# One visit to the values' products for four query blocks, with shared buffers in the first half

## The chip, the cores and the metric

The kernel runs on one core of a Trainium2 chip. The metric is the device time of one execution in microseconds (us); lower is better. Before the change the median of three runs is 1810.27 us (1809.09 to 1811.99).

## The reference, cut to what matters

The program is one layer of a hybrid decoder trunk on 1024 tokens of width 1024: an RWKV-7 branch, a stick-breaking attention, a cross-attention into 256 memory tokens, gates, an output projection and a convolutional feed-forward. The change touches the stick-breaking attention alone (8 heads of 64, blocks of 128 queries):

```python
for blk in range(t_len // SB_BLOCK):          # 8 blocks of 128 queries
    start = blk * SB_BLOCK; end = start + SB_BLOCK
    qb, kb, vb = q[:, :, start:end], k[:, :, :end], v[:, :, :end]
    z = jnp.einsum('bhqd,bhkd->bhqk', qb, kb) * scale
    mask = s_idx[None, :] < t_idx[:, None]
    log_1mb = jnp.where(mask, jax.nn.log_sigmoid(-z), 0.0)
    log_between = lax.cumsum(log_1mb, axis=3, reverse=True) - log_1mb
    attn = jnp.where(mask, jnp.exp(jax.nn.log_sigmoid(z) + log_between), 0.0)
    outs.append(jnp.einsum('bhqk,bhkd->bhqd', attn, vb))
```

The kernel uses that these weights telescope: it keeps the running products of 1 - sigmoid(z) and multiplies them with the differences of neighbouring values, so that a product with a plain causal triangle remains.

## The kernel before, in words

The method `sb_attn` (L895) runs 64 units: head pair p (4), head of the pair h2 (2), half of the blocks (0: blocks 0 to 3, 1: blocks 4 to 7), block in the half (4). Unit u works on query block b against (b+1)*128 keys. A unit passes four steps:

- `front` (L900): the products of queries and keys (two matrix products per 512 keys, hi and lo part) into a PSUM bank of the tag g, then ScalarE's sigmoid (L913) into a buffer sn of the tag at.
- `weigh` (L916): VectorE's scan (L919) in place over sn, the running product.
- `mid` (L921): TensorE transposes sn in blocks of 128x128 (L105) into g banks, and ScalarE copies them out (L931) into a second buffer of the tag at.
- `back` (L933): for two units at a time, TensorE multiplies the values' differences (64 columns as the stationary operand, so each product uses half of the array's columns) with the transposed weights. Unit i of the two writes the lower or upper 64 partitions of a PSUM bank py of the tag mm, so that the two can run side by side. Unit 1 of a visit has one key block more. When four blocks are done, ScalarE copies py out (L954, four instructions) and stores it.

The loop at L959 calls front(u), at even u back(u-4), then mid(u-2) and weigh(u). With `yield` it hands over to the filler: the program's large projections, one step per yield (six products of 512 columns into two mm banks, an eighth of a projection), woven in by `weave` (L1820) at a ratio of 1.03 to one. `pumped` (L1878) further mixes in the steps of `inverse` (L538), a long chain of VectorE multiplications and additions (L545, L547), which ends with eight-row stores from GpSimd's queue (L554).

Order. TensorE's instructions in this part are pinned to program order, as are VectorE's scans and the inverse's steps. ScalarE, GpSimd and the rest of VectorE are ordered by the tile scheduler from priorities and from when it believes operands to be ready, so an edit of the program order can move their instructions too. The pools hold: tag at, 7 buffers of 128x1024; mm, 4 PSUM banks; g, 4 PSUM banks; w4 (shown as w), 3 buffers; wr, wh and wl (raw, hi and lo part of a weight tile), 2 each.

The filler's gates matter below: when a gate's projection is done, ScalarE copies it out (L820), VectorE scales it (L821), and later `close` makes ScalarE apply a sigmoid in place (L824) and store it (L826). A weight tile is loaded by SP (L76), rounded by ScalarE (L80, wh) and its rest formed by GpSimd (L81, wl).

Of the kernel before, what the change touches and what calls it, by code (L numbers as in the profile page):

```python
# [49 lines left out]
class Trunk:  # L50
# [844 lines left out]
    def sb_attn(self, qk, need):  # L895
        nc = self.nc
        units = [(p, half, h2, half * 4 + bb) for p in range(4) for h2 in range(2) for half in range(2) for bb in range(4)]
        st = {}

        def front(u):  # L900
            p, half, h2, b = units[u]
            need(f"sb{p}")
            S, K, KL, nf = qk[p]
            W = (b + 1) * 128
            ts = slice(b * 128, (b + 1) * 128)
            sn = self.t4("at", n=1024)
            for w0 in range(0, W, 512):
                w1 = min(w0 + 512, W)
                pz = self.ps("g")
                self.mmul(pz[:, : w1 - w0], S[h2][:, ts], K[h2][:, w0:w1], start=True, stop=False)  # L910
                self.mmul(pz[:, : w1 - w0], S[h2][:, ts], KL[h2][:, w0:w1], start=False, stop=True)
                i = 2 * b + h2
                nc.scalar.activation(sn[:, w0:w1], pz[:, : w1 - w0], AF.Sigmoid, scale=nf[:, i : i + 1])  # L913
            st[u] = sn

        def weigh(u):  # L916
            W = (units[u][3] + 1) * 128
            sn = st[u]
            self.pinned(nc.vector.tensor_tensor_scan(sn[:, :W][:, ::-1], sn[:, :W][:, ::-1], self.nrt[:, 1152 - W :][:, ::-1], 1.0, ALU.mult, ALU.max))  # L919

        def mid(u):  # L921
            b = units[u][3]
            W = (b + 1) * 128
            at, sn = self.t4("at"), st[u]
            st[u] = at
            for w0 in range(0, W, 512):
                w1 = min(w0 + 512, W)
                pt = self.ps("g")
                for o in range(w0, w1, 128):
                    self.transpose(pt[:, o - w0 : o - w0 + 128], sn[:, o : o + 128])  # L930
                nc.scalar.activation(at[:, w0:w1], pt[:, : w1 - w0], AF.Copy)  # L931

        def back(u):  # L933
            p, half, h2, b = units[u]
            ats = [st.pop(u + i) for i in range(2)]
            if b % 4 == 0:
                st["py"] = self.ps("mm")
            py = st["py"]
            ts = slice(b % 4 * 64, b % 4 * 64 + 128)
            for j in range(b + 2):  # L940
                vo = (j % 2) * 512 + p * 128 + h2 * 64
                for i, at in enumerate(ats):
                    if j <= b + i:
                        self.mmul(
                            py[i * 64 : i * 64 + 64, ts], self.v[j // 2][:, vo : vo + 64], at[:, j * 128 : (j + 1) * 128],
                            start=(j == 0), stop=(j == b + i))
            if b % 4 == 2:
                q = slice(h2 * 64, h2 * 64 + 64)
                y = self.t4("ys", n=512)
                for i in range(2):  # L950
                    rows = slice(i * 64, i * 64 + 64)
                    for bb in range(2):
                        o, bi = (2 * bb + i) * 128, (2 * p + h2) * 4 + half * 2 + bb
                        nc.scalar.activation(  # L954
                            y[q, o : o + 128], py[rows, bb * 128 : bb * 128 + 128], AF.Identity,
                            bias=self.vlast[rows, bi : bi + 1])
                nc.scalar.dma_start(self.yd[1, p, q, half * 512 : (half + 1) * 512], y[q])

        for u in range(len(units) + 4):  # L959
            if u < len(units):  # L960
                front(u)
            if u % 2 == 0:
                yield
                if u >= 4:
                    back(u - 4)
            if 2 <= u < len(units) + 2:
                mid(u - 2)
            if u < len(units):
                weigh(u)
            yield  # L970
            if u % 2:
                yield
# [1017 lines left out]
```

## Time and profile before

| what | value |
|---|---|
| median of three runs | 1810.27 us |
| the profiled execution's own time | 1808.94 us |
| its span on the core | 1807.2 us |
| granted TensorE clock in it | 1.00 |
| TensorE busy | 1783.0 us, 99% of the span |
| VectorE, ScalarE, GpSimd busy | 65%, 48%, 44% |

The attention of the change lies between 324 and 634 us of the span. In the rows of the profile, PE is TensorE's products, PEld its weight loads, DVE VectorE, ACT ScalarE, POOL GpSimd, SP the engine that issues most transfers. A row of the timeline has the start, the length, the engine, the line, the operation, the tiles written and read, the shape, and in brackets the engine's idle time before it and what ended that. Lengths of overlapping products add up to more than the time that they take, so spacing between starts is what counts on PE.

### The profile page before, as it was taken

The page shows a single profiled execution, that of the slowest core. Times are in us where ns is not written, and L with a number is a line of the kernel's source. Part 1 is how long each engine was busy: PE and PEld are TensorE (multiplying, and loading weights), DVE is VectorE, ACT ScalarE, POOL GpSimd, SP SyncE. Part 2 cuts the span into 40 slices and gives each one's busy share as a digit, 9 for nine tenths or more (in the row PEclk, how much of TensorE's full clock was granted, in tenths as well). Part 3 has the DMA queues.
Part 4 walks back from the last instruction along what each step waited for, and adds up shares of the span by engine and source line. Part 5 has one row for each costly group of instructions (what it writes and reads, how often), then busy time and mean ns, then how long its engine had stood idle before and what let it go on. Part 6 is the DMA issues. An engine that isn't in the chain of part 4 may idle for free. (4 is left out here: it accounts for less than half of the span.)

```text
span 1807.2 us, 27322 instructions
## 1 busy us (share of the span) xinstructions
PE 1783.0 (99%) x10479; PEld 1440.4 (80%) x10479; DVE 1179.3 (65%) x1625; ACT 865.2 (48%) x1556; POOL 789.7 (44%) x448
## 2 busy tenths in 40 slices
PE   9999999999999999999999999989999999999998
PEld 7777778878788888777777878868888888888877
DVE  5667775898887625244443872587767777794586
ACT  6444344556566636544444334544444445454343
POOL 3223353322222462122422541487677677545454
PEclk9999999999999999999999999999999999999999
DMA  5155664211112352567654553223323333395475
GB/s 208 59 163 176 197 209 155 73 42 45 53 55 69 112 152 69 184 232 282 227 187 176 183 201 106 105 88 113 110 88 104 112 111 111 119 343 190 136 261 180
DMA packets 122628, 261.29 MB, mean 145 GB/s; under 512 B 28665, under 2 KB 43385, under 8 KB 122370
## 3 DMA queue, kind: packets, MB, share of 16 engines
q1 hardware_dynamic: 84882, 193.70, 32.4%
q10 hardware_dynamic: 33840, 53.23, 8.0%
q0 software_dynamic: 3776, 12.62, 2.2%
q8 instruction: 82, 1.34, 0.3%
q14 instruction: 48, 0.39, 0.1%
HBM read 178.99 MB, written 80.48 MB: 144 GB/s over the span
## 5 line engine op out<-in xcount | busy, mean ns | idle before, releaser
L81 POOL TENSOR_TENSOR wl<-wr,wh 128x1024 fp32r<-128x1024 f32 (+2 forms) x78 | 197.9, 2538 | 501.0 <-ACT wh L80 491.3
L115 PE MATMUL mm<-xhi,wh 128*128 128x512 f32 x784 | 260.5, 413 | 0.9 <-DVE w L322 0.4
L115 PE MATMUL mm<-xlo,wh 128*128 128x512 f32 x784 | 243.6, 392 | 0.2 <-DVE xlo L199 0.2
L115 PE MATMUL mm<-xhi,wl 128*128 128x512 f32 x784 | 242.5, 391 | 0.0
L115 PEld LDWEIGHTS mm<-xlo,wh 128*128 128x128 f32 x784 | 147.2, 188 | 33.5 <-DVE xlo L199 0.6
L115 PEld LDWEIGHTS mm<-xhi,wl 128*128 128x128 f32 x784 | 147.1, 188 | 33.0 <-POOL wl L81 0.7
L115 PEld LDWEIGHTS mm<-xhi,wh 128*128 128x128 f32 x784 | 136.8, 190 | 29.4 <-issue 6.1
L80 ACT ACTIVATE wh<-wr 128x1024 fp32r<-128x1024 f32 (+2 forms) x78 | 81.8, 1049 | 146.1 <-PE mm L115 85.1
L115 PE MATMUL mm<-dw,da 128*128 128x512 f32 x528 | 121.9, 390 | 1.5 <-DVE da L1727 1.3
L115 PE MATMUL mm<-BT,l 128*128 128x512 f32 x504 | 118.0, 389 | 1.6 <-POOL l L1457 1.6
L115 PEld LDWEIGHTS mm<-dw,da 128*128 128x128 f32 x528 | 98.7, 188 | 24.0 <-DVE da L1727 3.0
L1728 POOL TENSOR_TENSOR dw<-draw,dw 128x512 fp32r<-128x512 f32 x55 | 81.6, 1492 | 82.6 <-ACT dw L1726 81.3
L115 PEld LDWEIGHTS mm<-BT,l 128*128 128x128 f32 x504 | 94.5, 188 | 21.6 <-POOL l L1457 2.0
L115 PE MATMUL mm<-BT,wh 128*128 128x512 f32 x352 | 108.8, 390 | 1.6 <-DVE BT L1367 0.9
L919 DVE TENSOR_TENSOR_SCAN at<-at,nrt 128x128 f32<-128x128 f32 (+3 forms) x64 | 90.3, 1420 | 30.0 <-ACT at L913 29.6
L115 PE MATMUL mm<-B,wh 128*128 128x512 f32 x352 | 108.5, 389 | 0.0
L1727 DVE TENSOR_TENSOR da<-draw,da 128x512 fp32r<-128x512 f32 x77 | 63.6, 836 | 58.9 <-ACT da L1725 58.4
L115 PE MATMUL g<-dw,da 128*128 128x512 f32 x396 | 90.8, 390 | 2.2 <-POOL dw L1728 1.1
L1457 POOL TENSOR_TENSOR l<-it,l 128x1024 fp32r<-128x1024 f32 x21 | 50.8, 2417 | 92.2 <-ACT l L1454 92.2
L115 PEld LDWEIGHTS g<-dw,da 128*128 128x128 f32 x396 | 74.2, 188 | 18.3 <-ACT dw L1726 1.5
L1725 ACT ACTIVATE da<-draw 128x512 fp32r<-128x512 f32 x77 | 48.3, 628 | 81.7 <-PE mm L115 38.2
L821 DVE TENSOR_TENSOR w<-w,nrt 128x1024 f32<-128x1024 f32 x24 | 49.9, 2081 | 57.0 <-ACT w L820 46.0
(335 smaller groups left out, 3982.4 us busy)
## 6 DMA issues: line engine op xcount, KB each, us to landing
wr<-in_w_in_dram SPq DMA_DIRECT2D x48, 512.0 KB, 3.6
draw<-actd SPq DMA_DIRECT2D x77, 256.0 KB, 3.2
draw<-in_w_down_dram SPq DMA_DIRECT2D x55, 256.0 KB, 4.4
at<-scr SPq DMA_DIRECT2D x24, 512.0 KB, 5.8
wr<-in_w_up_dram SPq DMA_DIRECT2D x22, 512.0 KB, 3.5
actd<-gall ACTq DMA_DIRECT2D x44, 256.0 KB, 3.1
rw<-in_w_up_dram SPq DMA_DIRECT2D x20, 512.0 KB, 3.7
gsd<-w ACTq DMA_DIRECT2D x18, 512.0 KB, 2.7
```

The lines of the kernel that those rows point to most:

```text
L80: self.nc.scalar.activation(hi, raw, AF.Copy)
L81: self.nc.gpsimd.tensor_tensor(lo, raw, hi.bitcast(F32), ALU.subtract)
L115: self.pinned(self.nc.tensor.matmul(*a, **k))
L821: nc.vector.tensor_tensor(g, g, self.nrb, ALU.mult)
L919: self.pinned(nc.vector.tensor_tensor_scan(sn[:, :W][:, ::-1], sn[:, :W][:, ::-1], self.nrt[:, 1152 - W :][:, ::-1], 1.0, ALU.mult, ALU.max))
L1457: nc.gpsimd.tensor_tensor(lo, src, hi.bitcast(F32), ALU.subtract)
L1725: self.pinned(nc.scalar.activation(A[:, 0], a, AF.Copy))
L1727: self.pinned(nc.vector.tensor_tensor(A[:, 1], a, A[:, 0].bitcast(F32), ALU.subtract))
L1728: nc.gpsimd.tensor_tensor(Wt[:, 1], w, Wt[:, 0].bitcast(F32), ALU.subtract)
```

## The change

A visit to the values' products now handles four units instead of two: at every second even step the units u-6, u-5 and u-4, u-3, in two calls of `back` right behind one another, where before each even step had one call. The units of half 0, whose blocks are at most 512 wide, share buffers of the tag at by twos: an even unit takes a buffer and uses its left half, the odd one behind it the right half, both for sn ("s") and for the transposed weights ("a"). No product, copy or scan is added or taken away.

```diff
+        def shared(kind, u):
+            if units[u][1]:
+                return self.t4("at")
+            if u % 2 == 0:
+                st[kind] = self.t4("at")
+            return st[kind][:, u % 2 * 512 : u % 2 * 512 + 512]
+
         def front(u):
...
-            sn = self.t4("at", n=1024)
+            sn = shared("s", u)
...
         def mid(u):
...
-            at, sn = self.t4("at"), st[u]
+            at, sn = shared("a", u), st[u]
...
             if u % 2 == 0:
                 yield
-                if u >= 4:
+                if u >= 6 and u % 4 == 2:
+                    back(u - 6)
                     back(u - 4)
```

TensorE, the first visit, step u = 4. Before, between a filler step (mm from xhi, xlo) and the three transposes of unit 2:

```order
L115 MATMUL mm_2788<-xhi_129,wl_2676 128x512
L115 MATMUL mm_2789<-xhi_129,wl_2676 128x512
L115 MATMUL mm_2797<-at_2731,A_2276 64x128
L115 MATMUL mm_2797<-at_2748,A_2276 64x128 x2
L105 MATMUL g_2802<-kon,at_2716 128x128 x3
L115 MATMUL mm_2788<-xhi_145,wh_2675 128x512
```

Now, at the same place and at step u = 6 behind it:

```order
L115 MATMUL mm_2785<-xhi_129,wl_2676 128x512
L115 MATMUL mm_2786<-xhi_129,wl_2676 128x512
L105 MATMUL g_2795<-kon,at_2715 128x128 x3
L115 MATMUL mm_2785<-xhi_145,wh_2675 128x512
...
L115 MATMUL mm_2786<-xhi_232,wl_2676 128x512
L115 MATMUL mm_2853<-at_2730,A_2276 64x128 x3
L115 MATMUL mm_2853<-at_2794,A_2276 64x128 x4
L115 MATMUL mm_2853<-at_2794,A_2279 64x128 x3
L105 MATMUL g_2871<-kon,at_2770 128x128 x4
```

The three products of blocks 0 and 1 have moved behind the next filler steps and stand directly ahead of the seven of blocks 2 and 3; at_2730 and at_2794 hold two units each. All 16 visits of steps 4, 8, 12 and so on move in this way, and nothing else changes its place on TensorE.

ScalarE, around the third gate of this part (w_707 before, w_691 now; lines behind L905 have numbers higher by 7 in the changed kernel, so L913 is L920, L931 is L938 and L954 is L961). Before:

```order
L820 ACTIVATE w_707_4058<-mm_3882 128x512
L820 ACTIVATE w_707_4058<-mm_3883 128x512
L913 ACTIVATE at_4064<-g_4065,nf_3945 128x128
L824 ACTIVATE w_707_4058<-w_707_4058 128x1024
L931 ACTIVATE at_4096<-g_4097 128x512
L931 ACTIVATE at_4096<-g_4103 128x384
L826 DMA gsd<-w_707_4058 128x1024
L913 ACTIVATE at_4115<-g_4116,nf_3945 128x256
```

Now:

```order
L820 ACTIVATE w_691_4042<-mm_3867 128x512
L820 ACTIVATE w_691_4042<-mm_3868 128x512
L920 ACTIVATE at_4048<-g_4049,nf_3925 128x128
L938 ACTIVATE at_4068<-g_4069 128x512
L938 ACTIVATE at_4068<-g_4075 128x384
L824 ACTIVATE w_691_4042<-w_691_4042 128x1024
L826 DMA gsd<-w_691_4042 128x1024
L920 ACTIVATE at_4048<-g_4087,nf_3925 128x256
```

The two copies of transposed weights have moved ahead of the gate's sigmoid. The same move stands at five gates of this part (those whose copies start at 398.68, 433.55, 475.81, 512.05 and 551.52 us in the profile before). At two places, where the keys of a head pair are split, a copy L863 and later an L864 have moved ahead of four L954 and of two L871; near the end an L80 has moved ahead of two L913.

GpSimd, near the end of this part, where the memory's norm is formed (rm, L171). Before:

```order
L81 TENSOR_TENSOR wl_5130<-wr_5127,wh_5129 128x1024
L81 TENSOR_TENSOR wl_5332<-wr_5329,wh_5331 128x1024
L171 TENSOR_TENSOR rm_5396<-rs_5397,half 128x2
L81 TENSOR_TENSOR wl_5405<-wr_5402,wh_5404 128x1024
L81 TENSOR_TENSOR wl_5459<-wr_5456,wh_5458 128x1024
```

Now:

```order
L81 TENSOR_TENSOR wl_5102<-wr_5099,wh_5101 128x1024
L81 TENSOR_TENSOR wl_5301<-wr_5298,wh_5300 128x1024
L81 TENSOR_TENSOR wl_5369<-wr_5366,wh_5368 128x1024
L171 TENSOR_TENSOR rm_5360<-rs_5361,half 128x2
L81 TENSOR_TENSOR wl_5427<-wr_5424,wh_5426 128x1024
```

One weight rest has moved ahead of rm; on VectorE a scan of 768 columns (L919) has moved likewise ahead of the multiplication that needs rm (L1005). SP's queue has the same order as before.

## The prediction

> **What bounds the kernel.** I read the first part of the profile page, then the windows of 40 us over the attention, then the waits of PE, then PE's timeline around the visits.
>
> ```profile
> PE 1783.0 (99%) x10479; PEld 1440.4 (80%) x10479; DVE 1179.3 (65%) x1625; ACT 865.2 (48%) x1556; POOL 789.7 (44%) x448
> ```
>
> In the windows, behind start, end and length, stand the busy times of PE, PEld, DVE, ACT and POOL, then the granted clock, the DMA share and GB/s.
>
> ```profile
> 404.00:444.00 40.00, 40.00 (x300) 32.88 (x299) 31.00 (x27) 20.70 (x41) 9.54 (x4) 1.00 0.15 47
> 444.00:484.00 40.00, 37.05 (x253) 30.08 (x253) 38.71 (x32) 25.49 (x46) 10.84 (x4) 1.00 0.14 46
> ```
>
> PE is the bound, at the full clock (1.00): it never stops from 404 to 444 us, while the others have room. Only from 444 to 484 us does it lose time, and there DVE has 38.71 of 40 us busy. So two things count: what PE spends beyond its products, and what it waits for. The waits of PE in this part (sum, number, longest):
>
> ```profile
> PE g L105 <- ACT at L931: 3.9, 3, 2.9
> PE mm L115 <- POOL wl L81: 1.7, 1, 1.7
> PE mm L115 <- ACT w L871: 0.4, 1, 0.4
> ```
>
> **What a visit costs beyond its products.** A visit puts products of 64 columns between products of 128.
>
> ```profile
> 334.64 0.61 PE L115 MATMUL mm<-xlo,wh 128*128 128x512 f32 x2
> 335.09 0.61 PE L115 MATMUL mm<-xhi,wl 128*128 128x512 f32 x2
> 335.64 0.66 PE L115 MATMUL mm<-at,A 128*64 128x128 f32 x6
> 336.23 0.55 PE L105 MATMUL g<-kon,at 128*128 128x128 f32 x3
> 336.53 0.71 PE L115 MATMUL mm<-xhi,wh 128*128 128x512 f32 x2
> ...
> 338.67 0.60 PE L105 MATMUL g<-kon,at 128*128 128x128 f32 x4
> 339.03 0.72 PE L115 MATMUL mm<-xhi,wh 128*128 128x512 f32 x2
> ...
> 344.16 1.09 PE L115 MATMUL mm<-at,A 128*64 128x128 f32 x14
> 345.19 0.77 PE L105 MATMUL g<-kon,at 128*128 128x128 f32 x5
> ```
>
> Going by starts: two products of 512 take 0.45 (334.64 to 335.09), but 0.55 ahead of the visit, so **entry** costs 0.10. Inside, 6 records take 0.59 and 14 take 1.03 us. The two units of a visit run side by side, so the longer one counts: 4 and 8 slots. Four slots more cost 0.44, or 0.11 each; 4 slots are 0.44, and 0.15 is **fixed** (8 slots give 0.88 + 0.15 as well). Behind the visit three transposes take 0.30, elsewhere four take 0.36, or 0.27 for three: 0.03 at the **exit**. A visit costs 0.10 + 0.15 + 0.03 = 0.28 us beyond its products.
>
> [...]
>
> **The merged visits.** Of 32 visits 16 lose their entry and exit. Fourteen lie ahead of 608 us: 14 x 0.28 = 3.9 us. One more stands behind other products of 64 columns:
>
> ```profile
> 351.76 1.10 PE L115 MATMUL g<-kon,w 128*64 128x2 f32 x32
> 352.72 1.51 PE L115 MATMUL mm<-at,A 128*64 128x128 f32 x22
> ```
>
> Its entry is paid by these 32, which stay: only the exit goes, 0.03. The last is in the tail, below. At the junction inside a merged visit (of 6 + 14 or 22 + 30 records) the next products wait for nothing, since another bank is written. Against that, the shorter unit's slack there may not close up: 0 to 0.05 each, and I take 0. **Sum: -4.0 us** (-3.3 with 14 x 0.05). The buffers cost no wait: at most seven are live, as many as the tag has, and each is freed by a PE instruction that stands ahead of those whose result fills it.
>
> **The gates' waits.**
>
> ```profile
> 472.90 0.60 PE L105 MATMUL g<-kon,at 128*128 128x128 f32 x4
> 476.44 0.66 PE L105 MATMUL g<-kon,at 128*128 128x128 f32 x4 [2.94 <-ACT at L931]
> ```
>
> ```profile
> 474.85 1.06 ACT L824 ACTIVATE w<-w 128x1024 f32<-128x1024 f32 x1 [5.38 <-DVE w L821]
> 475.81 0.58 ACT L931 ACTIVATE at<-g 128x512 f32<-128x512 f32 x1
> ```
>
> ```profile
> 461.20 1.28 DVE L882 SCALAR_TENSOR_TENSOR qk<-w,params,qk 64x1024 fp32r<-64x1024 f32 x1
> ...
> 466.77 2.29 DVE L919 TENSOR_TENSOR_SCAN at<-at,nrt 128x1024 f32<-128x1024 f32 x1
> 469.09 3.38 DVE L882 SCALAR_TENSOR_TENSOR qk<-w,params,qk 64x1024 fp32r<-64x1024 f32 x1
> ```
>
> ```profile
> 469.03 2.36 POOL L81 TENSOR_TENSOR wl<-wr,wh 128x1024 fp32r<-128x1024 f32 x1
> ```
>
> ACT's queue is in order. The gate's sigmoid L824 waits 5.38 us for the gate's scaling L821, which is late behind an L882 that takes 3.38 beside a POOL weight rest, and 1.28 alone. Behind L824 stand two copies L931, which free the g banks, and for them PE waits 2.94. Now these copies stand ahead of L824 at all five gates, and nothing that they read comes late: **-3.9 us**, the whole row. Behind L824 then stands a sigmoid L913, and the scan that follows it has time to spare: the one at 466.77 ends at 469.06, 3.84 ahead of its transposes (472.90). The third wait,
>
> ```profile
> 373.72 0.50 PE L115 MATMUL mm<-xhi,wh 128*128 128x512 f32 x1 [0.37 <-ACT w L871]
> ```
>
> is for an mm bank; as no py holds one between the two old visits, I let it go: **-0.4** (0 if it stays). What is late next is DVE: from 444 to 484 us it has 1.29 us idle, so if PE gains 2.94 there, DVE's backlog of scans shrinks from 3.84 to about 0.9, just enough. New small waits follow from the reordering (an L863 and L864 ahead of L871 and L954, an L80 ahead of two L913). No row shows them; between 0 and 2.4, one weight rest (2.36) in full, I take **+0.8**, what a 128x2 operation waited for POOL in the row at 609.60 below.
>
> **The tail.**
>
> ```profile
> 621.07 1.53 PE L115 MATMUL mm<-at,A 128*64 128x128 f32 x22
> 622.53 0.98 PE L105 MATMUL g<-kon,at 128*128 128x128 f32 x7
> ...
> 627.09 0.40 PE L115 MATMUL mm<-qk,wh 128*128 128x256 f32 x2
> 629.18 0.39 PE L115 MATMUL mm<-qk,wl 128*128 128x256 f32 x1 [1.69 <-POOL wl L81]
> ...
> 632.01 1.97 PE L115 MATMUL mm<-at,A 128*64 128x128 f32 x30
> ```
>
> ```profile
> 625.81 0.91 POOL L554 DMA_DIRECT2D td<-inst  x1 [3.02 <-PE g L105]
> 626.75 4.71 POOL L81 TENSOR_TENSOR wl<-wr,wh 128x1024 fp32r<-128x1024 f32 x2
> ```
>
> ```profile
> 608.64 0.16 DVE L170 TENSOR_SCALAR rs<-g 128x2 f32<-128x2 f32 x1 [0.85 <-PE g L115]
> 609.60 2.35 DVE L1005 TENSOR_TENSOR rm<-rm 128x2 f32<-128x2 f32 x1 [0.81 <-POOL rm L171]
> ...
> 612.25 1.75 DVE L919 TENSOR_TENSOR_SCAN at<-at,nrt 128x768 f32<-128x768 f32 x1
> ...
> 625.24 0.28 DVE L547 TENSOR_TENSOR inst<-inst,it 128x62 f32<-128x62 f32 x1
> ```
>
> At 629.18 PE waited 1.69 for a weight rest. That stood behind the store L554 in POOL's queue, and the store came right behind the inverse's last step (625.24 + 0.28). The visit of 22 records at 621.07 lies ahead of this wait, and now goes behind it. PE gets there 1.46 + 0.10 + 0.03 = 1.6 us sooner and waits 1.6 longer; the visit at 632.01 grows by 12 slots, 1.3 us. So the last merge **costs 1.3**. The DVE chain starts from PE at 608.64, so it moves forward with all that PE gains before. It also gains by order: the scan of 1.75 now fills the 0.81 that DVE idled ahead of L1005, **-0.8**. At best L1005, slow beside the weight rest that ran then, also drops from 2.35 to the 0.16 of L170, another 2.2: -3.0. At worst rm, behind one rest of 2.4, comes so much later and the scan hides 1.75: +0.7.
>
> **Sum:** -4.0 - 3.9 - 0.4 + 0.8 + 1.3 - 0.8 = -7.0. The profiled execution took 1808.94, so 1801.9; the median is 1.33 above it, so **1803.3**. Bounds: -4.0 - 3.9 - 0.4 + 0 + 1.3 - 3.0 = -10.0, and -3.3 - 3.9 + 0 + 2.4 + 1.3 + 0.7 = -2.8: by the median 1800.3 to 1807.5, and 1798.9 from the profiled execution.
>
> **Rivals.**
>
> *B, the gate waits only change place*: DVE, full from 444 to 484 us, holds PE where ACT did, or the copies are held by something else. For: 1.29 us idle. Against: the scans' 3.84. Without -4.3 the sum is -2.7: 1807.6.
>
> *C, the tail takes the gain*: if POOL's rest before 629.18 isn't moved forward by PE's gain (the chain hangs on its own work, DVE being nearly full), all that PE gains before is waited for there, and only +1.3 is left: 1811.6. Against: the 0.85 that DVE waited for PE at 608.64.
>
> *D, slower*: the collision at the gates moves. L882 took 3.38 because the rest on POOL had started 0.06 us before it; whether they meet is chance, and of five gates one made PE wait 2.9. If with PE earlier they meet at four, and the bank is now held by the L913 behind L824, PE waits 2.9 four times, 11.6 instead of 3.9: -4.0 - 0.4 + 7.7 + 0.8 + 1.3 - 0.8 = +4.6, or 1814.9. It decides from three such gates. Against: the L913 is one bank where the two L931 were two of four.
>
> [...]
>
> *E, the merge saves nothing*: the cost of 0.28 comes from each unit's bank and not from the change of columns. Then -4.0 goes and the tail costs 1.6: -4.3 + 0.8 + 1.6 - 0.8 = -2.7, 1807.6. Against: the same 0.15 for 6 and 14 records.
>
> **How the numbers follow.** Forecast 0.67, B 0.14, C 0.08, D 0.06, E 0.05. About 0.2% (3.6 us) is what a measurement of this kernel can tell from no change: below 1806.65 is faster, above 1813.9 slower. The forecast is faster (0.67), B, C and E are the same (0.27), D is slower (0.06). The range leaves out C and D: it starts at 1798.9 and ends with B when the new waits are 2.4, 1807.6 + 1.6 = 1809.2.
>
> **What would show it.** Right: 16 visits of 20 and 52 records, 12 and 28 slots long, with 1.47 and 3.23 us (slots x 0.11 + 0.15) to the next product; no PE wait on the transposes' copy, which then stands ahead of L824; a wait of about 2.5 where 1.69 stood at 629.18; 320 to 600 us shorter by about 8 us. Wrong: PE waits for DVE's scans between 460 and 490 us (B), a wait of 9 us or more at the weight rest (C), waits of 2 to 3 us at several gates for L913's line (D), or merged visits of 1.6 and 3.4 us (E).

## The result, and the profile after

| | before | changed |
|---|---|---|
| median, 13 runs each | 1812.16 us | 1807.54 us |
| lowest to highest | 1809.09 to 1813.86 | 1805.33 to 1808.74 |
| ratio, with 95% interval | | 0.9975 (0.9968 to 0.9983) |
| the profiled execution's own time | 1808.94 us | 1807.54 us |
| its span | 1807.2 us | 1805.8 us |

The change makes the kernel 0.25% faster, 4.6 us by the medians, where 7.0 were forecast. The two profiled executions differ by 1.4 us only: the one before lies below each of its 13 runs, and the experiments show a part of why (the entry on copy_before).

The page's first part for the changed kernel, and the window from 444 to 484 us with the columns of before:

```profile
PE 1779.9 (99%) x10479; PEld 1442.8 (80%) x10479; DVE 1178.7 (65%) x1625; ACT 864.3 (48%) x1556; POOL 789.1 (44%) x448
```

```profile
444.00:484.00 40.00, 38.82 (x268) 31.78 (x267) 37.36 (x31) 25.89 (x52) 10.66 (x4) 1.00 0.16 50
```

From 444 to 484 us PE has 38.82 us busy instead of 37.05: the wait at the gate is gone from this window, but 1.18 us are still idle. The list of PE's waits (sum, number, longest) says on what:

```profile
PE mm L115 <- POOL wl L81: 2.3, 1, 2.3
PE g L115 <- ACT at L920: 2.1, 3, 1.0
PE g L115 <- DVE hn L766: 0.9, 1, 0.9
PE g L105 <- DVE hn L766: 0.4, 1, 0.4
PE g L105 <- ACT at L938: 0.2, 1, 0.2
```

The waits of 3.9 for the transposes' copy (L931, now L938) have shrunk to 0.2, and the 0.4 for L871 is gone. New are 2.1 for the sigmoid of `front` (L920) and 1.3 in two waits put down to L766, a VectorE line of the woven-in work. The wait at the weight rest has grown from 1.7 to 2.3.

**The visits.** PE's timeline around two merged visits, of 20 and of 52 products:

```profile
607.37 1.53 PE L115 MATMUL mm<-at,A 128*64 128x128 f32 x20
608.83 0.77 PE L105 MATMUL g<-kon,at 128*128 128x128 f32 x5
...
627.99 3.28 PE L115 MATMUL mm<-at,A 128*64 128x128 f32 x52
631.19 0.50 PE L115 MATMUL mm<-qk,wh 128*128 128x256 f32 x2
```

From start to start 1.46 and 3.20 us, where 1.47 and 3.23 were forecast.

**The gate** that cost 2.94 us before, in PE's and then in ACT's timeline:

```profile
470.34 0.40 PE L115 MATMUL g<-qk,qk 128*128 128x256 f32 x2
470.57 1.04 PE L105 MATMUL g<-kon,at 128*128 128x128 f32 x8
```

```profile
468.82 0.98 ACT L938 ACTIVATE at<-g 128x512 f32<-128x512 f32 x2
...
472.82 1.06 ACT L824 ACTIVATE w<-w 128x1024 f32<-128x1024 f32 x1 [3.02 <-DVE w L821]
```

The sigmoid L824 still waits 3.02 us for L821, but the copies stand ahead of it, at 468.82, and the eight transposes at 470.57 run without a stop.

**A ledger of the way.** The table holds, for a few units of the attention, when the unit's first transposes start, less the same start in the profiled execution before (negative: earlier). It is worked out from the timelines' rows at the transposes' line, and shows where each kernel gains or loses. The kernels do not start level: at unit 0 these rows already stand between -0.18 and +0.43 (the change at -0.03, kq_ordered at +0.33). So a difference between two rows is good to about half a microsecond, and a step within a row is surer. The other kernels belong to the experiments below.

| unit (start before, us) | 12 (383.1) | 24 (443.0) | 28 (460.9) | 32 (484.8) | 44 (539.4) | 48 (560.5) | 60 (613.3) | 63 (624.8) |
|---|---|---|---|---|---|---|---|---|
| the change | -1.29 | -2.19 | -0.72 | -4.16 | -3.78 | -3.88 | -4.48 | -6.07 |
| copy_before | | | -0.16 | +1.45 | | | +1.37 | +1.37 |
| tail_old | -1.08 | -1.98 | -0.52 | -4.00 | -3.61 | -3.72 | -4.31 | -4.31 |
| kq_ordered | -0.93 | -2.96 | -3.24 | -6.74 | -7.60 | -8.32 | -8.91 | -10.51 |
| kq_tail_old | -1.40 | -3.44 | -3.72 | -7.22 | -8.08 | -8.80 | -9.36 | -9.36 |
| orders_only | -0.66 | -1.81 | -1.81 | -5.01 | -5.01 | -1.03 | -1.47 | -1.47 |
| kq_before | | | +0.29 | +2.35 | +2.34 | +6.02 | +5.99 | +5.99 |

In the row of the change, steps of about -0.3 are visits, the step of -3.44 from unit 28 to 32 is the gate with one visit, and the steps upwards (+1.47 at unit 28, +0.97 up to unit 44) are the new waits. (Unit 63 lies ahead of the last visit in kernels that merge it, so -6.07 is lent: at 642 us the change is 2.69 us ahead, tail_old 5.18, kq_ordered 7.14, kq_tail_old 10.31.)

**Where the new waits come from.** PE's rows with a wait, in the changed kernel:

```profile
385.29 0.73 PE L115 MATMUL g<-qk,qk 128*128 128x512 f32 x2 [0.88 <-DVE hn L766]
...
451.68 0.51 PE L115 MATMUL g<-qk,qk 128*128 128x256 f32 x2 [1.01 <-ACT at L920]
...
527.12 0.51 PE L115 MATMUL g<-qk,qk 128*128 128x256 f32 x2 [0.95 <-ACT at L920]
536.68 0.33 PE L105 MATMUL g<-kon,at 128*128 128x128 f32 x1 [0.37 <-DVE hn L766]
```

ACT's queue ahead of the second of them, in the changed kernel and then at the same place before:

```profile
447.00 1.06 ACT L864 ACTIVATE qk<-w 64x1024 fp32r<-64x1024 f32 x1
447.96 1.05 ACT L871 ACTIVATE w<-mm 128x512 f32<-128x512 f32 x2
449.04 1.06 ACT L80 ACTIVATE wh<-wr 128x1024 fp32r<-128x1024 f32 x1
450.01 1.04 ACT L872 ACTIVATE w<-w 128x1024 f32<-128x1024 f32 x1
450.95 0.93 ACT L920 ACTIVATE at<-g,nf 128x512 f32<-128x512 f32 x2
```

```profile
452.04 0.93 ACT L913 ACTIVATE at<-g,nf 128x512 f32<-128x512 f32 x2
...
453.38 1.06 ACT L864 ACTIVATE qk<-w 64x1024 fp32r<-64x1024 f32 x1
```

ACT works from 447.00 to 450.95 on a split, copies and a weight's rounding that the attention does not need at once, and only then on the sigmoid that empties the g banks; PE waits 1.01 for it. Before, the split L864 came after the sigmoid. Here one split of 1.06 at the wrong place on ACT is about one microsecond of PE.

A wait costs somewhat more than its row shows. Beside kq_ordered (below), where these waits are absent, the change falls back by 1.15 us at the wait of 0.88 (units 12 to 13), by 1.29 at that of 1.01 (26 to 27) and by 1.23 at that of 0.95 (42 to 43).

**The tail.** PE, then DVE, then POOL, in the changed kernel:

```profile
623.69 0.58 PE L115 MATMUL mm<-qk,wl 128*128 128x256 f32 x1 [2.28 <-POOL wl L81]
...
627.18 0.40 PE L115 MATMUL mm<-qk,wh 128*128 128x256 f32 x2
```

```profile
603.85 3.31 DVE L926 TENSOR_TENSOR_SCAN at<-at,nrt 128x768 f32<-128x768 f32 x1
607.68 0.16 DVE L1013 TENSOR_TENSOR rm<-rm 128x2 f32<-128x2 f32 x1 [0.52 <-POOL rm L171]
...
619.75 0.28 DVE L547 TENSOR_TENSOR inst<-inst,it 128x62 f32<-128x62 f32 x1
```

```profile
620.34 0.91 POOL L554 DMA_DIRECT2D td<-inst  x1 [3.02 <-DVE inst L547]
621.28 4.68 POOL L81 TENSOR_TENSOR wl<-wr,wh 128x1024 fp32r<-128x1024 f32 x2
```

The inverse's last step starts at 619.75 instead of 625.24, 5.49 earlier, and the rest behind its store moves with it, while PE at unit 60 is 4.48 earlier: the chain gains 1.0 on PE, where 0.8 was forecast. PE waits 2.28. Behind that wait comes what was not forecast. The rows from 629.18 to 631.20 took 2.02 before; the same products now take 3.49 (623.69 to 627.18). The window there, of the changed kernel and then of one without the long wait (tail_old, below):

```profile
623.60:627.00 3.40, 3.31 (x15) 3.31 (x16) 0.00 (x0) 0.00 (x0) 3.12 (x3) 0.50 0.51 164
```

```profile
623.80:627.20 3.40, 3.31 (x30) 3.18 (x32) 0.00 (x0) 0.81 (x3) 3.19 (x3) 1.00 0.52 155
```

The granted clock is 0.50 for about 3.4 us, and PE does 15 products where it does 30 at 1.00.

### The profile page after: what moved, and what is told of

The parts are those of the page before. It is cut to its first block, busy times and chain, and to the rows that moved or that the text cites. A ratio compares the mean times of both kernels' runs of the same rounds, so it can differ in the third digit from the quotient of the medians.

```text
span 1805.8 us, 27326 instructions
## 1 busy us (share of the span) xinstructions
PE 1779.9 (99%) x10479; PEld 1442.8 (80%) x10479; DVE 1178.7 (65%) x1625; ACT 864.3 (48%) x1556; POOL 789.1 (44%) x448
## 4 chain that ended last, share of the span: by engine, by line
PE 66%; DVE 7%; issue 3%; DMA 3%; ACT 3%; POOL 2%; ACTq 0%; DVEq 0%; POOLq 0%; SPq 0%
PE mm L115 55%; PE g L115 8%; PE g L105 3%; DMA wr<-in_w_out_dram 1%; DVE at L926 1%; DVE it L545 1%; POOL wl L81 1%; DMA A<-yd 1%; DVE da L1735 1%; DVE at L1287 0%; DVE mg L1294 0%; DVE inst L547 0%; DMA dx<-x2d 0%; DMA out_dram<-dx 0%; ACT at L1143 0%
## 5 line engine op out<-in xcount | busy, mean ns | idle before, releaser
L80 ACT ACTIVATE wh<-wr 128x1024 fp32r<-128x1024 f32 (+2 forms) x78 | 81.8, 1048 | 146.8 <-PE mm L115 94.5
L926 DVE TENSOR_TENSOR_SCAN at<-at,nrt 128x128 f32<-128x128 f32 (+3 forms) x64 | 94.2, 1478 | 25.5 <-ACT at L920 25.3
L821 DVE TENSOR_TENSOR w<-w,nrt 128x1024 f32<-128x1024 f32 x24 | 49.8, 2076 | 58.5 <-ACT w L820 47.6
```

Of the source, the lines that this page charges most:

```text
L80: self.nc.scalar.activation(hi, raw, AF.Copy)
L821: nc.vector.tensor_tensor(g, g, self.nrb, ALU.mult)
```

## The experiments

The theory behind the first ones: visits and gates do what was forecast, what is missing was lost on ACT's new order (the splits) and at the last merged visit. The rivals are that the visits save less, that the shared buffers cost, or that what is gained is waited for later on. Each kernel's time stands beside that of the kernel before, taken along with it. `self.ordered(x)` keeps an instruction in program order among those of its engine that are so marked.

### after_again: the change, unaltered

> The changed kernel unaltered, for a second profile. Theory (a ledger of five terms): from 324 to 600 us its TensorE gains 4.5 us on the profile of before again (0.30 for each of 14 merged visits is 4.2; 4.0 for the gates' waits; 3.4 given back in new waits behind the splits of keys and queries and a norm), the wait for the weight rest near 623 us is 2.3 us again, and the 1.75 us that it lost near 1046 us in the first profile need not come again. Rival (the loss near 1046 belongs to the change, since TensorE arrives there sooner than the weights): 1.5 us or more is lost there again. Time: 0.9975 of before, 0.9968 to 0.9983.

1808.24 us against 1811.35, ratio 0.9978 (0.9969 to 0.9987). The gain is there again: from unit 0 to unit 60 TensorE gains 4.5, as expected. What was lost near 1046 us came again, against the theory: from 642 to 1062 us it loses 2.67, so the rival is not refuted. The new waits stand at the same places, and the wait at the weight rest (2.27) is again followed by a low clock, 0.57.

### share_only: the shared buffers with the old visits

```diff
-                if u >= 6 and u % 4 == 2:
-                    back(u - 6)
+                if u >= 4:
                     back(u - 4)
```

> The shared buffers alone, with 32 visits of two units as before. Theory: nothing but the visits moved ScalarE's order and saved time, so this is the kernel before: within 0.1% of it, with the waits for the transposes' copies (3.9 us in sum) still there. Rival (the buffers, freed by twos, gave part of the gain): 1.5 us or more faster, and the gates' waits shorter.

1811.92 us, ratio 1.0004 (0.9994 to 1.0013). In its trace the wait for the copies at the gate stays:

```profile
476.53 0.85 PE L105 MATMUL g<-kon,at 128*128 128x128 f32 x4 [2.56 <-ACT at L938]
```

Its copies still start behind L824 (475.89 behind 474.93). So sharing the buffers by itself is worth nothing, and it is not what moved ACT's copies ahead of L824. The move of PE's visits, the only other part of the edit, did that.

### gates_behind: the kernel before, with the copies held ahead of the gates

```diff
-                nc.scalar.activation(g, g, AF.Sigmoid, scale=-1.0)
+                c = nc.scalar.activation(g, g, AF.Sigmoid, scale=-1.0)
+                if b != 2 and 2 <= d <= 6:
+                    self.ordered(c)
```

The copies L931 of block 6 are marked likewise.

> The kernel before, with the gates' sigmoid held behind the copies of transposed weights of unit 6 of each eight, as the merge happened to put it; the visits stay at 32. Theory: TensorE's waits for the copies fall from 3.9 us to 0.3 or less, and the kernel is 2 to 3.7 us faster (up to 1.5 of it may come back in new waits of the splits, whose order moves at one place too). Rival (VectorE sets the pace from 444 to 484 us, the copies were only where it showed): the waits move to VectorE's scans or norms, and the time is the same within 1 us.

1809.77 us against 1811.35, ratio 0.9987 (0.9979 to 0.9996): 1.6 us, less than expected. By unit 32 it is 4.75 us ahead. The waits of 0.37 (for L871), 0.73 and 2.94 that the kernel before has up to there are gone; they sum to 4.0, and each costs some 0.2 more than its row. So the gates do pay what the forecast said. Then a new wait takes most of it back:

```profile
549.95 0.66 PE L105 MATMUL g<-kon,at 128*128 128x128 f32 x4 [2.60 <-ACT at L933]
```

So the mechanism of the gates held, with its size up to unit 32; that their repair leaves other places as they were did not.

### tail_old: the change, with the last four units in two visits

```diff
-                if u >= 6 and u % 4 == 2:
+                if u >= len(units):
+                    back(u - 4)
+                elif u >= 6 and u % 4 == 2:
                     back(u - 6)
                     back(u - 4)
```

> The change without its last merge: the last four units in two visits as before, 15 merges of 16. Theory: the visit of 22 records is hidden again in the wait for the weight rest, which falls from 2.3 to about 0.7 us; the last visit is 1.3 us shorter, and the granted clock stays 1.00 behind so short a wait (1.5 us): 2.8 us faster than the change, 0.9960 of before. Rival (the wait only follows what GpSimd does, and the clock falls by chance): no more than 1.3 us faster than the change, and the clock falls again.

1805.65 us, ratio 0.9966 (0.9954 to 0.9977): 2.6 us less than after_again, beside 2.8 expected. With the visit of 22 products back ahead of the weight rest the wait is short, and the clock stays at 1.00 (the window above):

```profile
623.89 0.39 PE L115 MATMUL mm<-qk,wl 128*128 128x256 f32 x1 [0.71 <-POOL wl L81]
```

The last merge costs, as forecast, and costs twice: 1.3 us of work moved behind a wait, and the low clock behind the longer wait.

### kq_ordered: the change, with the splits held in program order

The two copies of `k_split` (L863, L864), those of `q_fin` (L871) and its square (L872) are marked:

```diff
-            nc.scalar.activation(K[i][o], kr[q], AF.Copy)
+            self.ordered(nc.scalar.activation(K[i][o], kr[q], AF.Copy))
```

> The change with ScalarE's splits of the keys (L863, L864) held in the order of the program, that is behind the copies and the square of the queries (L871, L872). Theory (the new waits of 1.0, 0.95 and 0.17 us near 451, 527 and 446 us come from an L864 that the merge put ahead of L871 to L913): these three go, the change becomes 2.1 us faster (0.9965 of before), less what new order there costs (up to 1). Rival (VectorE, nearly full in this stretch, holds TensorE anyway): the waits move to its scans or norms and the time stays within 0.7 us of the change.

1803.17 us against 1811.61, ratio 0.9949 (0.9936 to 0.9961): 5.1 us less than after_again, more than twice the 2.1 expected. ACT around the place of the 1.01 wait, and PE there:

```profile
446.92 1.06 ACT L872 ACTIVATE w<-w 128x1024 f32<-128x1024 f32 x1
447.87 0.94 ACT L920 ACTIVATE at<-g,nf 128x512 f32<-128x512 f32 x2
...
449.22 1.06 ACT L863 ACTIVATE qk<-w 64x1024 fp32r<-64x1024 f32 x1
```

```profile
448.80 0.85 PE L115 MATMUL g<-qk,qk 128*128 128x512 f32 x4
...
619.25 0.39 PE L115 MATMUL mm<-qk,wl 128*128 128x256 f32 x1 [2.27 <-POOL wl L81]
```

The splits now stand behind the sigmoid, and PE no longer waits there. All five new waits are gone, also the two put down to L766, which were DVE's. The edit marks only ACT's instructions, but DVE's order moved with it: ahead of the wait of 0.88, L766 (at 385.06) stood behind an L882 of 1.28 us in the change, and in kq_ordered it stands ahead of it (383.86). So part of this gain came through DVE's order, which the edit did not set. In this part of the program only 0.23 us at 579.72 and the wait at the weight rest are left. The expectation had counted only the waits for ACT.

### rest_first and combo: an attempt on the store ahead of the weight rest

The store L554 of the inverse was to be held behind two weight rests on POOL, by marking the first store and the rests, with six empty steps put in ahead of the stores. `combo` has the edits of kq_ordered as well.

```diff
-            nc.gpsimd.tensor_tensor(lo
+            c = nc.gpsimd.tensor_tensor(lo
...
+            if self.late:
+                self.ordered(c)
```

> The change with GpSimd's first store of the inverse (L554) held behind the weight rest for which TensorE waits near 623 us; all 16 merges stay. Theory: the wait of 2.3 us there falls below 0.3, with it the low clock behind it (1.5 us) goes, and the last merge gains its 0.3 as the others do: 3.5 to 4 us faster than the change, 0.9955 of before. Rival (the next thing is late too: the rest's weights or the stores, which stage 2 reads): at most 1.5 us faster, with a new wait of TensorE between 623 and 700 us.

> The two orders together on the change (key splits behind the queries' copies, first store behind the weight rest). Theory: the two gains add, since they lie 75 us apart and TensorE is the bound between them: 5 to 6 us faster than the change, 0.9945 of before. Rival (what TensorE gains before 640 us is waited for near 1040 us, where the out-projection's weights land): no faster than the better of the two.

1808.55 us, 0.9982 (0.9972 to 0.9992), and 1802.97 us, 0.9949 (0.9937 to 0.9962): neither differs from its base. The edit missed its aim: only the store named first was held, others moved ahead of the rest, and PE still waits:

```profile
624.17 0.39 PE L118 MATMUL mm<-qk,wl 128*128 128x256 f32 x1 [2.32 <-POOL wl L82]
```

(Lines are higher by 3 and by 1 there.) The two say nothing on what the store costs. They say something on the clock: behind these 2.32 it stayed at 1.00 in both.

### kq_store_behind: all stores of the inverse behind the rests

As combo, with every store L554 marked and without the six empty steps.

> kq_ordered with all of GpSimd's stores of the inverse (L554) held behind the weight rests of the memory's keys; rest_first had left the first store ahead of the rest in question, and only put the norm's square root back ahead of another one. Theory (the store makes the rest late, the last merge pays for it): no wait above 0.3 near 619 us, no low clock there, and 3.5 to 4 us faster than kq_ordered: 0.993 of before. Rival (the rest is late for its weights or for its buffers): a wait of 1 us or more stays within 10 us of that place, and at most 1.5 us are won.

1810.79 us, ratio 0.999 (0.9982 to 0.9999): 7.6 us slower than kq_ordered. PE, then POOL:

```profile
618.62 0.39 PE L118 MATMUL mm<-qk,wl 128*128 128x256 f32 x1 [1.62 <-POOL wl L82]
...
707.71 2.42 PE L118 MATMUL g<-A,qk 128*128 128x256 f32 x12 [3.35 <-ACT at L1151]
```

```profile
615.72 0.53 POOL L572 MEMSET it<- 128x512 f32 x1 [2.78 <-DVE inst L551]
...
703.72 2.35 POOL L82 TENSOR_TENSOR wl<-wr,wh 128x1024 fp32r<-128x1024 f32 x1 [10.63 <-ACT wh L81]
706.03 0.20 POOL L780 TENSOR_TENSOR hf<-hf,rsc 128x8 f32<-128x8 f32 x1
```

and the DVE operation that waits for the last of these:

```profile
706.26 0.23 DVE L1148 SCALAR_TENSOR_TENSOR nb<-mxt,hf 128x2 f32<-128x2 f32 x2 [9.26 <-POOL hf L780]
```

The store is gone from ahead of the rest, but the next stage's memset (L572), into a buffer that the inverse uses, stood there instead and waited 2.78 us for the inverse. So the wait stayed, as in the rival, but not for its reason (late weights or buffers): the rest starts right behind the memset, at 616.20. POOL's queue waits for the inverse through the memset as well as through the store. The time is lost further on: from 700 to 750 us PE falls from 9.1 us ahead of the kernel before to 2.3. At 707.71 it waits 3.35 for ACT's exponential in the cross-attention (L1151), which waits for DVE, and DVE waits for L780, a small operation of a norm on POOL. L780 stands behind a weight rest that waits 10.63 for its rounded weights; in kq_ordered the same operation is done by 695.24, and PE has no such wait. The late stores are not in this chain, the last of them having ended at 687.93; what holding them back costs by itself is not shown.

### copy_before: the kernel before, unaltered

> The kernel before unaltered, for a second profile of it: its first one took 1808.94 us and lies below all 13 runs of the first comparison (median 1812.16). Theory: the median execution loses the other 3 us to what that profile happened not to have, a granted clock of about 0.5 for some 3.4 us behind a wait of 2.5 us or more (1 to 1.5 us each), and weights that land later near 1040 or 1600 us. Rival (the profile's own execution differs in the attention part): TensorE is more than 1 us later by 460 us already.

1812.42 us, ratio 1.0003 (0.9994 to 1.0012), and a second profile of the same program. PE's row at the gate and the window behind it, here:

```profile
476.29 0.84 PE L105 MATMUL g<-kon,at 128*128 128x128 f32 x4 [3.02 <-ACT at L931]
```

```profile
476.25:479.75 3.50, 3.46 (x11) 2.88 (x12) 3.47 (x5) 1.70 (x4) 0.00 (x0) 0.55 0.37 150
```

and the window at the same place in the first profile before:

```profile
476.40:479.90 3.50, 3.46 (x17) 2.94 (x18) 3.46 (x5) 1.71 (x4) 0.00 (x0) 1.00 0.37 150
```

At 460 us TensorE is not later than in the first profile (ledger: -0.16), so the rival fell. The same wait, 3.02 and 2.94, is followed once by a clock of 0.55 and once by 1.00. The low clock costs 1.6 us by unit 32 (ledger: -0.16 to +1.45). So the profile that the forecast was made from had been spared: its execution took 1808.94 us, that of copy_before 1810.74. That is 1.8 of the 3.2 us by which the first lies below the median of 1812.16; the rest is open.

### kq_before: the kernel before, with the splits held in order

The edit of kq_ordered, without the change.

> The kernel before with the key splits held behind the queries' copies, as in kq_ordered, visits unmerged. Theory (what kq_ordered won are waits that only the merge's order had made): the three waits for the transposes' copies stay (3.9 us), and the time is that of before within 0.1%. Rival (the order of the splits is a gain by itself, and has nothing to do with the merge): 3 us or more faster than before.

1815.9 us against 1811.65, ratio 1.0022 (1.0013 to 1.0031): slower, where no difference was expected. The splits in order leave L824 ahead of the copies, and the gates get worse. PE, then ACT:

```profile
477.17 0.66 PE L105 MATMUL g<-kon,at 128*128 128x128 f32 x4 [3.44 <-ACT at L931]
...
556.59 0.86 PE L105 MATMUL g<-kon,at 128*128 128x128 f32 x4 [2.29 <-ACT at L931]
```

```profile
475.57 1.06 ACT L824 ACTIVATE w<-w 128x1024 f32<-128x1024 f32 x1 [5.96 <-DVE w L821]
```

Both waits are followed by a low clock (0.67 and 0.54). The same edit is worth -5.1 us on the changed kernel and +4.2 on the kernel before.

### kq_tail_old: the change, with the splits in order and the old tail

> kq_ordered with the last four units in two visits again. Theory (the two gains lie at different places and TensorE is the bound between): 2.6 us faster than kq_ordered, as tail_old was against the change: 0.9934 of before, some 1800.5 where before is 1811.6; the wait near 619 us 0.7 instead of 2.3 and the clock 1.00 behind it. Rival (what TensorE gains is waited for near 1040 us): no faster than kq_ordered.

1800.31 us (1798.96 to 1801.84), ratio 0.9936 (0.9924 to 0.9949): 2.9 us less than kq_ordered, beside 2.6 expected, and 11.3 below the kernel before (1811.65 beside it). It beats both kernels. In this part PE waits only twice:

```profile
579.24 0.66 PE L105 MATMUL g<-kon,at 128*128 128x128 f32 x4 [0.23 <-ACT at L938]
...
618.84 0.39 PE L115 MATMUL mm<-qk,wl 128*128 128x256 f32 x1 [0.71 <-POOL wl L81]
```

### orders_only: the kernel before with both orders, and the old visits

The edits of gates_behind and of kq_ordered together.

> The kernel before with both orders of ScalarE and no merge: the gates' sigmoid held behind the copies (as gates_behind, whose wait of 2.6 us near 550 us stays) and the key splits behind the queries' copies. Theory (the merge itself is worth 0.3 us for each visit taken away, whatever the order): against kq_tail_old TensorE falls back by 0.3 us for each of its 14 merges up to 600 us, 4.2, and by 2.6 near 550; 6.8 us slower in all, some 1807, 0.9974 of before; by 480 us, seven merges in, it is 2.1 behind kq_tail_old. Rival (the order of the splits pays only with the merge, as kq_before was slower than before): no better than gates_behind, 0.9987 of before, with new waits for copies or sigmoids ahead of 480 us.

1807.42 us against 1812.68, ratio 0.9974 (0.9963 to 0.9985), as expected. So the order of ACT's instructions alone, with all 32 visits, brings as much as the whole change. What kq_tail_old has beyond it by unit 32, -7.22 against -5.01, is 2.2 us, eight merged visits at 0.28. Behind that orders_only loses 4.0 us to a wait of 2.62, which no kernel with the change has, and to the low clock (0.56) that follows it. ACT, then PE:

```profile
546.37 1.06 ACT L985 ACTIVATE w<-w 128x1024 f32<-128x1024 f32 x1 [3.04 <-DVE qk L882]
```

```profile
549.55 0.79 PE L105 MATMUL g<-kon,at 128*128 128x128 f32 x4 [2.62 <-ACT at L931]
```

It is the mechanism of the gates at another line: an in-place operation that waits for DVE stands ahead of the copies.

## Why the prediction was right, and where it was off

The sign was right, and so were the mechanisms of the visits, of the gates and of the wait in the tail; the price of the new waits was not. The measured median, 1807.54, lies in the range, 4.2 us above the forecast. Of these, 1.9 belong to the starting point, as the median before is 1812.16 over 13 runs and not 1810.27 over three; the other 2.3 are in the difference, 4.6 measured against 7.0. The measured time is also the one that the rivals B and E had named (1807.6). So the number alone does not decide between them and the forecast; the ledger and the experiments do.

- **The visits, -4.0: right.** From unit to unit each merged visit shifts the ledger by 0.28 to 0.31. At 0.30, fourteen give 4.2. orders_only beside kq_tail_old, with the same orders, gives 0.28 per visit.
- **The gates' waits, -3.9, and L871's, -0.4: right.** In kq_ordered, where the new waits are gone, the ledger reaches -8.91 at unit 60; less 4.2 for the visits it is 4.7 (5.0 from its own start at unit 0), somewhat more than the 4.3 of the rows, as a wait costs more than its row. One part was misread: the third wait in the row of 3.9, 0.24 at 589.94, stands at a gate that is not among the five, where the copies stay behind L824. 0.23 of it is left in the change. DVE, named as late next, did not become the bound: no row of PE waits for a scan, and the backlog was enough.
- **The new waits, +0.8: the term that failed.** The forecast had seen an L863 and an L864 move ahead of L871 and L954, and priced the move with what a tiny operation had once waited for POOL; it bounded it by one weight rest, 2.4. The new waits listed add up to 3.4 (2.1, 0.9 and 0.4), and the change is behind kq_ordered by 4.4 at unit 60, which is more than the bound as well. (From each kernel's start it is 4.8: the five waits, each with some 0.3 beyond its row.) The error was to price the places together with one number. A split of about 1 us moves ahead of a sigmoid that frees a g bank, and there are several such places, each of which can reach PE, some of them by way of DVE. The rows of ACT needed for this were in the trace before: 1.06 for a split, 1.05 for two copies of 512.
- **The last merge, +1.3, and DVE's order, -0.8: right in what moved, wrong by what followed.** The wait is 2.28 where about 2.5 was forecast, the last visit takes 3.20, and the small operation behind rm came down to 0.16, as the best case had it; but the scan took 3.31 instead of 1.75. From unit 60 to 642 us the change loses 1.8 where +0.5 was forecast. 1.47 of it are the low clock behind the wait, which had no term; the 0.3 that is left lies near the forecast. tail_old takes the low clock and the cost of the merge away and gains 2.6 by the timed runs.
- **A gain that was not forecast, about -1.6:** in three of four profiles with a wait of 2.5 to 3.5 us near 476 us a low clock followed it (copy_before 0.55, share_only 0.55, kq_before 0.67; not the first profile before, 1.00). The kernels with merged visits have neither. Here luck helped: without this gain the time would have been, as an estimate, 1807.54 + 1.6 = 1809.1, at the upper end of the range (1809.2).

The terms as measured, -4.2 - 4.7 + 4.4 + 1.8, make the ledger's -2.69 at 642 us; they must, since the last three are differences of the ledger's own rows, and the first is taken off again in the second. Only the visits (from the steps) and the low clock (1.47, from its rows) are measured by themselves. From there to 1062 us the change gives back 1.25, which leaves the -1.4 between the two profiles. With the low clock at 476 us that the first profile before was spared (-1.6) it is -3.0; the other 1.6 of the 4.6 us by the medians have no row, as the profiled execution before was quick by more than this one event.

What is lost between 642 and 1062 us differs from run to run: 2.67 in after_again and 3.0 in kq_tail_old, 0.5 in kq_ordered and 0.3 in tail_old. In the change ACT waits longer there for weights to land (7.98 instead of 6.48 us at the load of the output projection), and PE waits 1.44 for DVE at 1047.13. In after_again a low clock (0.60), behind a wait of 1.63 at 1036.75, is part of it. Being ahead alone doesn't bring it: kq_ordered was 7.1 us ahead, and gates_behind, 2.1 ahead at 642 us, loses 2.9. Whether the lead has a part, or the loads vary from execution to execution, is not settled.

The rivals. **B**, in which the gates' waits only change place, holds in part: they were removed (gates_behind, kq_ordered), but the change itself gives back about as much through ACT's splits. It was given DVE as the place, and that fell. **C** fell: PE waits 2.28 at the weight rest and not 9. **D** fell for the change, where the L882 near the gate of 476 us starts 0.45 us ahead of POOL's weight rest and takes 1.28 (at 467.07; before, 0.06 behind it, 3.38 at 469.09). kq_before shows something like it in another kernel, two gates of 3.44 and 2.29, with the copies L931 (not an L913) behind L824, and slower by 0.22%. **E** fell by the visits' 0.28 to 0.31, though its time is the one measured.

## What to carry to other kernels

When an edit moves instructions on the bound engine, a scheduler may reorder other engines' instructions that nobody touched; list each place where something now stands ahead of the instruction that frees a bank, and price each by itself with the moved instruction's own time. Pinning such an order pays or costs depending on the others (here -5.1 and +4.2 us for the same four lines), so it has to be tried on the kernel in which it is to stay. Don't merge work across the one point where the bound engine waits anyway: here the visit of 22 products was hidden ahead of the wait at the weight rest, and behind it was not (tail_old, which leaves it ahead, is 2.6 us faster, the low clock's part included).

## What was not expected of the hardware

**The clock behind a wait.** Over all profiles, PE's waits of 2.27 to 3.44 us were followed by a granted clock of 0.52 to 0.67 over some 3.5 us in 9 of 13 cases (8 of 12 in this part, and the one at 707.71 in kq_store_behind), and by 1.00 in 4 (2.94, 2.32, 2.32 and 2.60 us long). Of 25 waits of 0.71 to 1.70 us between 320 and 645 us none was followed by a low clock. Later in the program some shorter ones were: one of 1.63 us in after_again (0.60), and near 1750 us two waits of about 1 us, 1.6 us apart, in 6 of the 14 profiles (0.51 to 0.68 behind the second). There it cost nothing in the end: kq_ordered fell from 6.4 to 4.9 us ahead of the kernel before, and was 6.2 ahead again by 1800 us, without the wait of 1.03 for DVE that the kernel before has at 1784.38. The same program has it in one execution and not in another (copy_before). Where PE was the bound it added about 1.5 us (1.47 in the change, 1.6 in copy_before), so the wait of 2.28 us in the change cost nearly 4, as an estimate (2.28 + 1.47).

**One profile can be the lucky one.** The execution that the forecast is made from lay 3.2 us below the median of 13 runs, of which one such event is about half; the change was worth 4.6.
